# Banded attention heads of a two-layer trunk: values as weights in two column halves, both query groups in one unit

## The chip, the cores and the metric

One core of a Trainium2 chip runs the whole program. The metric is the device time of one execution in microseconds (us), the median of three runs. The core has a matrix engine (TensorE, PE in the profile; PEld is its weight load), a vector engine (VectorE, DVE), an activation engine (ScalarE, ACT), GpSimd (POOL), and a queue that issues the transfers (SyncE, SP). Operands lie in SBUF; TensorE writes its results to PSUM banks of 128 x 512 floats.

## The reference

A diffusion trunk of two layers over 256 latent tokens (x) and 256 context tokens (h). Each layer is a SwiGLU sub-layer, a token mixing with three groups of heads, and a second SwiGLU sub-layer, each between norms whose shifts, scales and gates come from conditioning vectors.

```
uv_x, qb_x, qc_x, kb_x, vb_x, kc_x, vc_x = jnp.split(ax @ w_in[l], SPLITS, axis=-1)
...
o_a = chunk_gmlp(uv_x, gmlp_v_gain[l], gmlp_w_s[l], gmlp_b_s[l])
o_b = diff_post(diff_attention_latent(qb_x, k_all, v_all, lam), diff_subln[l], lam_init)
o_c = swa_latent(qc_x, kc_x, vc_x, kc_h, vc_h, sink)
mix_x = jnp.concatenate([o_a, o_b, o_c], axis=-1) @ w_out[l]
x = adaln_out(x, mix_x, norm_post[l, 1], mod_x[:, 5], 1.0)
```

The change is in o_c, the banded heads: four query heads of 64 columns, head kv*2+g with two key/value heads kv and two query groups g. A latent query block of 128 tokens reads 512 keys (latent and context), a context block the 256 context keys. A sink logit joins each softmax. In the last layer only the latent tokens are mixed.

## The kernel before

Weights come from HBM through a staging ring of three tiles (`stg`) and are split into a rounded part and its remainder (`hi` by ACT, L240; `lo` by DVE or POOL, L101). Products of split operands take three passes of TensorE: L250 and L254 where weights are stationary and tokens move, L263, L269 and L271 in `acc3_multi`, with tokens stationary in the output projection. Full-precision products (scores, transposes, probabilities times values) use plain float32 tiles; one such matmul leaves two records in the trace, a transpose one.

The mixing is written as a long main line of projections and output products, into which small units are interleaved. A unit is a generator: it emits some instructions, then yields a delay on a virtual clock that counts TensorE columns (`tick`), and goes on when the clock has passed the delay. `T_SOFT`, `T_SOFTC` and `T_TURN` are such delays, and `pace` spaces the starts. A scheduler then fixes one order for each engine; at run time each engine takes its own order strictly in turn.

`unit_c(tb, g, box)` handles token block tb and group g: scores of kv 0 and 1 (L865, contraction over 64 rows), mask, row maximum (L874), exponential with row sum (ACT, L876), the sink's exponential (L878), reciprocal; after T_SOFT, `soft_T` turns each probability tile in 128x128 pieces (L781, copied to SBUF by L783); after T_TURN, L895 multiplies with the turned probabilities stationary (128 columns of weights) and 64 columns of values moving, and ACT copies the result, scaled by the reciprocal, into its quarter of `oc` (L899). When both groups of a block are through, `finish_c` turns `oc` (L1010), and writes Yh and Yl, the split operand of the output projection, rows 6 and 7 (L1014, L1015).

There are four blocks in layer 0 (tb 2 and 3 with 256 keys, tb 0 and 1 with 512) and two in layer 1 (512 keys). `unit_b` (L797, L781, L818) does the same for the differential heads, `post_b` (L846, L850, L851) their norm and turn. `spatial` (L929) is the gated group: two matmuls with 64-column weights write the two partition halves of one bank. `done` and `residual` (L1082, L1083, L422, L439, L444, L447) follow an output block of 128 tokens; `turn_y` (L461, L466, L471) makes the input of the next sub-layer.

Ring of six tiles of 512 columns, tag "p": probabilities, gate temporaries, gate rows, and more; ring of seven tiles of 256 columns, tag "sq". PSUM: four `pa`, two `pb`, two `pc` banks.

Of the kernel before, what the change touches and what calls it, by code (L numbers as in the profile page):

```python
# [37 lines left out]
T_SOFT, T_SOFTC, T_TURN, T_POST = 4.5, 3.5, 1.5, 3.0  # L38
# [25 lines left out]
def trunk(ctx: ExitStack, tc: tile.TileContext, x, c, cx, c_ctx, w_mod, b_mod, norm_pre, norm_post,  # L64
# [623 lines left out]
    def mixing(l, streams, qstreams, nxt):  # L688
# [166 lines left out]
        def unit_c(tb, g, box):  # L855
            k0, k1 = keys_of(tb)
            n = k1 - k0
            nkb = n // P
            mx = sm.tile([P, 2], F32, tag="mx", name=nm("mx"))
            ss = sm.tile([P, 4], F32, tag="ss4", name=nm("ss"))  # L860
            rs = sm.tile([P, 2], F32, tag="rs", name=nm("rs"))
            sc = [pa(), pa()]
            p = [half("p"), half("p")]
            for kv in range(2):
                nc.tensor.matmul(sc[kv][:, 0:n],  # L865
                                 lhsT=CU[64 * kv:64 * kv + 64, 1 + g, tb * P:(tb + 1) * P],
                                 rhs=CU[64 * kv:64 * kv + 64, 0, k0:k1], start=True, stop=True)
# [11 lines left out]
            nc.vector.tensor_tensor(rs, ss[:, 0:2], ss[:, 2:4], op=ALU.add)
            nc.vector.reciprocal(rs, rs)  # L880
            tick(1536)
            yield T_SOFT
            pT = []
            for kv in range(2):
# [6 lines left out]
            for kv in range(2):  # L891
                hd = kv * 2 + g
# [107 lines left out]
        def units_c(tb, w):  # L1000
            return [(2.0 * w, unit_c(tb, g, boxes[tb])) for g in range(2)]

        def finish_c(tb):
            while pending[("u", tb)]:
                yield 0.4
            oc = boxes[tb][0]
            yield T_TURN
            t = pa()
            for i in range(2):
                nc.tensor.transpose(t[:, i * P:(i + 1) * P], oc[:, i * P:(i + 1) * P], ident)  # L1010
# [318 lines left out]
```

## Time and profile before

| what | value |
|---|---|
| median of three runs | 1762.15 us (1761.32 to 1762.53) |
| profiled execution, time | 1762.98 us |
| profiled execution, span of its instructions | 1761.2 us |
| TensorE busy | 1722.4 us (98%) |
| VectorE busy | 1190.4 us (68%) |
| ScalarE busy | 696.3 us (40%) |
| mean granted TensorE clock | 0.997 |

The span runs from the first to the last instruction; the 1.8 us around it are start and end. Busy is the union of an engine's records. TensorE's matmuls overlap each other in the records, so that its pace is read from one start to the next. The mixing of layer 0 lies at some 465 to 640 us of the span, that of layer 1 at some 1455 to 1570 us.

### The profile page before, as it was taken

What the parts mean: (1) busy time and instruction counts of PE and PEld (TensorE: products, weight loads), DVE (VectorE), ACT (ScalarE), POOL (GpSimd) and SP (SyncE); (2) the same over time, 40 slices, a digit from 0 to 9 for tenths busy, and PEclk for the clock granted to TensorE, in tenths of its full rate; (3) what the DMA queues carried; (4) which work ended last, traced back from release to release, by engine and by line L of the source; (5) the groups of instructions that cost most, each with busy time, mean ns of one, the idle gap of its engine ahead of it and who ended that gap; (6) DMA issues with size and microseconds to landing.
All of it is one profiled execution on the core that took longest, in us unless ns stands there. A gap on an engine that the chain in (4) does not pass through costs nothing.

```text
span 1761.2 us, 24837 instructions
## 1 busy us (share of the span) xinstructions
PE 1722.4 (98%) x9663; PEld 1449.9 (82%) x9663; DVE 1190.4 (68%) x2174; ACT 696.3 (40%) x1480; POOL 168.9 (10%) x185
## 2 busy tenths in 40 slices
PE   7999999999999999999999999999999999999998
PEld 5788888879977789888888898888888897689997
DVE  4876876775667576768766576777864756765555
ACT  4332322244376562333232442332223526655443
POOL 0000000021322120000000210000001321010000
PEclk9999999999999999999999999999999999999999
DMA  9654554543131143445545233655544133226552
GB/s 336 207 173 160 188 197 144 167 150 109 60 103 52 57 137 125 162 163 189 191 144 185 75 120 123 205 178 191 180 144 167 48 108 120 73 90 197 192 191 84
DMA packets 197105, 259.20 MB, mean 147 GB/s; under 512 B 8234, under 2 KB 132348, under 8 KB 196988
## 3 DMA queue, kind: packets, MB, share of 16 engines
q1 hardware_dynamic: 195452, 257.56, 44.3%
q8 instruction: 76, 1.25, 0.3%
q14 instruction: 41, 0.34, 0.1%
q0 software_dynamic: 1536, 0.05, 0.0%
HBM read 256.49 MB, written 1.10 MB: 146 GB/s over the span
## 4 chain that ended last, share of the span: by engine, by line
PE 63%; DVE 7%; ACT 2%; issue 2%; POOL 1%; DMA 1%; POOLq 0%; DVEq 0%; ACTq 0%
PE pa L250 19%; PE pa L254 9%; PE pb L269 4%; PE pb L271 4%; PE pb L263 4%; PE pa L263 4%; PE pa L271 4%; PE pa L269 4%; PE pb L250 3%; DVE lo L101 2%; PE pb L254 1%; PE pa L797 1%; PE pc L818 1%; PE pc L895 1%; DVE S L439 1%
## 5 line engine op out<-in xcount | busy, mean ns | idle before, releaser
L101 DVE TENSOR_TENSOR lo<-stg,hi 128x512 fp32r<-128x512 f32 (+3 forms) x476 | 367.0, 807 | 192.5 <-ACT hi L240 122.8
L240 ACT ACTIVATE hi<-stg 128x512 fp32r<-128x512 f32 (+3 forms) x496 | 318.4, 702 | 329.6 <-PE pa L263 97.2
L250 PE MATMUL pa<-Yh,hi 128*128 128x512 f32 (+1 forms) x1168 | 415.0, 365 | 0.0
L250 PE MATMUL pa<-Yl,hi 128*128 128x512 f32 (+1 forms) x1168 | 413.8, 364 | 0.0
L357 DVE SCALAR_TENSOR_TENSOR acc<-stg,sT,acc 128x512 f32<-128x512 f32 x448 | 305.2, 743 | 4.0 <-DMA stg<-in_w_mod_dram 4.0
L254 PE MATMUL pa<-Yh,lo 128*128 128x512 f32 (+1 forms) x1168 | 257.8, 363 | 0.0
L250 PEld LDWEIGHTS pa<-Yh,hi 128*128 128x128 f32 x1168 | 220.5, 189 | 36.6 <-issue 2.9
L250 PEld LDWEIGHTS pa<-Yl,hi 128*128 128x128 f32 x1168 | 220.5, 189 | 35.0 <-issue 1.2
L254 PEld LDWEIGHTS pa<-Yh,lo 128*128 128x128 f32 x1168 | 202.4, 189 | 34.3
L570 ACT ACTIVATE Uh<-ha 128x512 fp32r<-128x512 f32 (+1 forms) x92 | 50.7, 551 | 296.4 <-DVE ha L568 296.4
L263 PE MATMUL pb<-hi,Ul 128*128 128x512 f32 x400 | 156.9, 392 | 0.0
L271 PE MATMUL pb<-lo,Uh 128*128 128x512 f32 x400 | 155.9, 390 | 0.8 <-DVE lo L101 0.8
L269 PE MATMUL pb<-hi,Uh 128*128 128x512 f32 x400 | 155.8, 391 | 0.1
L568 DVE TENSOR_TENSOR ha<-ha,pa 128x512 f32<-128x512 f32 (+1 forms) x91 | 53.0, 583 | 79.5 <-PE pa L254 79.0
L269 PE MATMUL pa<-Yh,hi 128*128 128x256 f32 x368 | 92.0, 285 | 0.0
L271 PE MATMUL pa<-Yl,hi 128*128 128x256 f32 x368 | 91.3, 283 | 0.0
L271 PEld LDWEIGHTS pb<-lo,Uh 128*128 128x128 f32 x400 | 75.1, 188 | 16.6 <-DVE lo L101 1.3
L263 PEld LDWEIGHTS pb<-hi,Ul 128*128 128x128 f32 x400 | 75.1, 188 | 16.5 <-issue 1.2
L269 PEld LDWEIGHTS pb<-hi,Uh 128*128 128x128 f32 x400 | 75.2, 188 | 16.0 <-DVE Z L503 0.5
L566 ACT ACTIVATE ht<-pa 128x512 f32<-128x512 f32 (+1 forms) x91 | 46.3, 510 | 104.1 <-PE pa L254 81.8
L379 POOL DMA_DIRECT2D gate<-gr x48 | 24.3, 513 | 603.7 <-DVE gr L376 535.3
L567 DVE SCALAR_TENSOR_TENSOR ha<-ht,pa 128x512 f32<-128x512 f32 (+1 forms) x91 | 52.9, 581 | 37.2 <-ACT ht L566 36.4
(299 smaller groups left out, 2732.4 us busy)
## 6 DMA issues: line engine op xcount, KB each, us to landing
stg<-in_w_mod_dram SPq DMA_DIRECT2D x64, 1024.0 KB, 5.0
stg<-in_ffn_w_gate_dram SPq DMA_DIRECT2D x42, 1024.0 KB, 5.2
stg<-in_ffn_w_up_dram SPq DMA_DIRECT2D x42, 1024.0 KB, 5.1
stg<-in_ffn_w_down_dram SPq DMA_DIRECT2D x32, 1024.0 KB, 5.0
stg<-in_w_in_dram SPq DMA_DIRECT2D x14, 1024.0 KB, 4.8
stg<-in_ffn_w_down_dram SPq DMA_DIRECT2D x16, 768.0 KB, 4.4
mst<-in_w_mod_dram SPq DMA_DIRECT2D x16, 512.0 KB, 7.6
stg<-in_w_out_dram SPq DMA_DIRECT2D x8, 1024.0 KB, 6.4
```

Of the source, the lines that this page charges most:

```text
L101: eng.tensor_tensor(lo, full, f32(hi), op=ALU.subtract)
L240: nc.scalar.activation(hi[:, a:b, :], v[:, a:b, :], AF.Copy)
L250: nc.tensor.matmul(o, lhsT=ah, rhs=r, start=(i == 0), stop=(i == n - 1))
L254: nc.tensor.matmul(o, lhsT=al, rhs=bh, start=(i == 0), stop=(i == n - 1))
L263: nc.tensor.matmul(o, lhsT=al, rhs=bh, start=False, stop=last, skip_group_check=True)
L269: nc.tensor.matmul(o, lhsT=ah, rhs=bh, start=(first and k == 0), stop=False, skip_group_check=True)
L271: nc.tensor.matmul(o, lhsT=ah, rhs=bl, start=False, stop=False, skip_group_check=True)
L357: nc.vector.scalar_tensor_tensor(a, v[:, k, :], sc, a, op0=ALU.mult, op1=ALU.add)
L566: nc.scalar.activation(t, g, AF.Tanh, scale=0.5)
L567: nc.vector.scalar_tensor_tensor(a, t, 1.0, g, op0=ALU.add, op1=ALU.mult)
L568: nc.vector.tensor_tensor(a, a, u, op=ALU.mult)
L570: nc.scalar.activation(uh, a, AF.Copy)
```

## The change

One unit now handles a block with both groups. It makes the four probability tiles, DVE multiplies each by its reciprocal (L885), and the turned pieces of both groups stand side by side in one PSUM bank (L896: two key blocks x two groups). Values are stationary with 64 columns, 256 columns of turned probabilities move (L903), and kv 0 and kv 1 write partitions 0 to 63 and 64 to 127 of one bank. The result is already turned, in the order (kv, d) by (g, token): the turning of `oc` falls away, and the rows of w_out that meet it are loaded in the same order, through two transfers of 64 partitions each (`out_stage`). gelu2's temporaries move from the "p" ring to the "sq" ring.

```diff
-T_SOFT, T_SOFTC, T_TURN, T_POST = 4.5, 3.5, 1.5, 3.0
+T_SOFT, T_SOFTC, T_TURN, T_POST = 4.5, 6.5, 1.5, 3.0
...
-        def unit_c(tb, g, box):
+        def unit_c(tb, w, box):
...
-            yield T_SOFT
-            pT = []
-            for kv in range(2):
-                pT.append(soft_T(p[kv], nkb))
-                tick(nkb * 288)
-            yield T_TURN
-            if not box:
-                box.append(wk.tile([P, 256], F32, tag="sq", name=nm("oc"), bufs=7))
-            oc = box[0]
-            for kv in range(2):
-                hd = kv * 2 + g
-                o = pc()
-                for kb in range(nkb):
-                    nc.tensor.matmul(o[:, 0:64], lhsT=pT[kv][:, kb * P:(kb + 1) * P],
-                                     rhs=VG[:, k0 // P + kb, 512 + kv * 64:512 + kv * 64 + 64],
-                                     start=(kb == 0), stop=(kb == nkb - 1))
-                tick(nkb * 320)
-                nc.scalar.activation(oc[:, hd * 64:hd * 64 + 64], o[:, 0:64], AF.Copy,
-                                     scale=rs[:, kv:kv + 1])
+                for kv in range(2):
+                    nc.vector.tensor_scalar(p[g, kv][:, 0:n], p[g, kv][:, 0:n], rs[:, kv:kv + 1], None,
+                                            op0=ALU.mult)
+                tick(1536)
+                yield T_SOFTC if g else w * pace[0]
+            o = pc()
+            for kb in range(0, nkb, 2):
+                pT = []
+                for kv in range(2):
+                    t = pa()
+                    for i in range(4):
+                        c0 = (kb + i // 2) * P
+                        nc.tensor.transpose(t[:, i * P:(i + 1) * P], p[i % 2, kv][:, c0:c0 + P], ident)
+                    pT.append(wk.tile([P, 512], F32, tag="a", name=nm("pT")))
+                    nc.scalar.activation(pT[kv], t, AF.Copy)
+                tick(2304)
+                yield T_TURN
+                for i in range(2):
+                    for kv in range(2):
+                        nc.tensor.matmul(o[64 * kv:64 * kv + 64, 0:256],
+                                         lhsT=VG[:, k0 // P + kb + i, 512 + kv * 64:576 + kv * 64],
+                                         rhs=pT[kv][:, i * 256:(i + 1) * 256], start=(kb + i == 0),
+                                         stop=(kb + i == nkb - 1))
+                tick(2560)
+            oc = wk.tile([P, 256], F32, tag="sq", name=nm("oc"), bufs=7)
+            nc.scalar.activation(oc, o[:, 0:256], AF.Copy)
+            box.append(oc)
...
-            xs, q = half("gx")[:, 0:n], half("gq")[:, 0:n]
+            xs, q = [wk.tile([P, 256], F32, tag="sq", name=nm(t), bufs=7) for t in ("gx", "gq")]
...
-            return [(2.0 * w, unit_c(tb, g, boxes[tb])) for g in range(2)]
+            return [(4.0 * w, unit_c(tb, 2.0 * w, boxes[tb]))]
...
+        def out_stage(blocks, c0, ncol):
...
+            nc.sync.dma_start(v[:, k0:k0 + n, :],
+                              w_out[l, r0:r0 + n * P, cs].rearrange("(k p) c -> p k c", p=P))
+            if 6 in blocks:
+                k0 = blocks.index(6)
+                for kv in range(2):
+                    r0 = (6 + kv) * P
+                    nc.sync.dma_start(v[64 * kv:64 * kv + 64, k0:k0 + 2, :],
+                                      w_out[l, r0:r0 + P, cs].rearrange("(g d) c -> d g c", g=2))
+            return v
```

**TensorE, layer 0, the first of the two 512-key blocks, before.** L865 is a score product, L895 probabilities times values of one kv, L781 a turn, L263 to L271 the output projection of the context tokens.

```order
L263 MATMUL pb_5257<-hi_5146,Yl 128x512
L865 MATMUL pa_5382<-CU_3759 128x512
L865 MATMUL pa_5383<-CU_3759 128x512
L269 MATMUL pb_5257<-hi_5146,Yh 128x512
L271 MATMUL pb_5257<-lo_5147,Yh 128x512
L895 MATMUL pc_5402<-VG_3223,pT_5367 128x64 x4
L895 MATMUL pc_5408<-VG_3223,pT_5374 128x64 x4
L781 MATMUL pa_5414<-ident,p_5326 128x128 x4
L781 MATMUL pa_5421<-ident,p_5327 128x128 x4
```

The same block in the changed order, its two groups of L903 (p_5196 and p_5256 are the probabilities of kv 0, p_5297 belongs to the next block; L939 is `spatial`):

```order
L903 MATMUL pc_5360<-pT_5366,VG_3223 64x256
L903 MATMUL pc_5360<-pT_5373,VG_3223 64x256
L903 MATMUL pc_5360<-pT_5366,VG_3223 64x256
L903 MATMUL pc_5360<-pT_5373,VG_3223 64x256
...
L896 MATMUL pa_5466<-ident,p_5297 128x128
L903 MATMUL pc_5360<-pT_5413,VG_3223 64x256
L939 MATMUL pc_5449<-wsT_3220,VG_3223 64x128 x2
...
L903 MATMUL pc_5360<-pT_5420,VG_3223 64x256
L903 MATMUL pc_5360<-pT_5413,VG_3223 64x256
L903 MATMUL pc_5360<-pT_5420,VG_3223 64x256
```

Two sets of eight 64-column products per block became two groups of four 256-column products. The first group stands together; in the second one product stands alone and three follow later.

**ScalarE, layer 0, the second 512-key block, after.** L879 is the exponential of a probability tile, L881 the sink's, L898 the copy of a turned bank; p_5297 and p_5299 are the first group of the second block, p_5380 and p_5382 the other group.

```order
L879 ACTIVATE p_5297,ss_5293<-pa_5295,mx_5292 128x512
L881 ACTIVATE ss_5293<-sink_3202,mx_5292 128x1
L898 ACTIVATE pT_5366<-pa_5361 128x512
L898 ACTIVATE pT_5373<-pa_5368 128x512
L881 ACTIVATE ss_5376<-sink_3202,mx_5375 128x1 x2
L879 ACTIVATE p_5299,ss_5293<-pa_5296,mx_5292 128x512
L879 ACTIVATE p_5380,ss_5376<-pa_5378,mx_5375 128x512
L898 ACTIVATE pT_5413<-pa_5408 128x512
```

The second exponential of the first group stands behind the sink exponentials of the other group.

**TensorE, layer 1, from the last scores of the second block on, before.** L846 turns the differential heads' output; the last row is the first of the second output block and needs their Yh.

```order
L865 MATMUL pa_13283<-CU_12221 128x512
L865 MATMUL pa_13284<-CU_12221 128x512
L781 MATMUL pa_13301<-ident,p_13216 128x128 x4
L781 MATMUL pa_13308<-ident,p_13217 128x128 x4
L263 MATMUL pb_13188<-hi_13017,Yl 128x256
L263 MATMUL pb_13188<-Yh,Yl 128x256 x6
L846 MATMUL pa_13322<-ident,CU_12221 128x128 x4
L263 MATMUL pb_13188<-Yh,Yl 128x256 x2
L895 MATMUL pc_13353<-VG_11787,pT_13306 128x64 x4
L781 MATMUL pa_13365<-ident,p_13285 128x128 x4
L781 MATMUL pa_13372<-ident,p_13286 128x128 x4
L895 MATMUL pc_13359<-VG_11787,pT_13313 128x64 x4
...
L269 MATMUL pb_13396<-hi_12837,Yh 128x512
```

And after, where L868 is the score product:

```order
L868 MATMUL pa_13228<-CU_12171 128x512
L263 MATMUL pb_13130<-hi_12905,Yl 128x256
L263 MATMUL pb_13130<-Yh,Yl 128x256 x7
L846 MATMUL pa_13255<-ident,CU_12171 128x128 x4
L263 MATMUL pb_13130<-Yh,Yl 128x256
L896 MATMUL pa_13285<-ident,p_13152 128x128
L896 MATMUL pa_13292<-ident,p_13154 128x128
L269 MATMUL pb_13349<-hi_12789,Yh 128x512
L271 MATMUL pb_13349<-lo_12790,Yh 128x512
...
L271 MATMUL pb_13349<-lo_12790,Yh 128x512
L896 MATMUL pa_13285<-ident,p_13229 128x128
```

The eight products and sixteen turns that stood between the last scores and the second output block are two turns now. Between the two pieces shown, 15 products of 256 columns and 3 of 512 follow, then the first turn of the other group, p_13229.

**VectorE, layer 1, the same stretch, after.** L422 to L447 are the residual and norm of the first output block, L885 the new multiplication.

```order
L422 SCALAR_TENSOR_TENSOR v_13268<-ss_12927 128x1
L1099 TENSOR_TENSOR zg_13263<-pb_13130,VG_11737 128x512
L439 SCALAR_TENSOR_TENSOR S<-zg_13127,r_13269,S 128x512
L439 SCALAR_TENSOR_TENSOR S<-zg_13263,r_13269,S 128x512
L882 TENSOR_TENSOR rs_13226<-ss_13225 128x2
L851 SCALAR_TENSOR_TENSOR Yl<-pa_13255,gsub_5771,Yh 128x4x128
L883 RECIPROCAL rs_13226<-rs_13226 128x2
L422 SCALAR_TENSOR_TENSOR v_13277<-ss_13274 128x1
L885 TENSOR_SCALAR p_13229<-p_13229,rs_13226 128x512
```

The multiplication of p_13229 stands behind the residual and behind a second L422.

**ScalarE, layer 1, start of the last sub-layer, before** (L240 splits a weight tile, the last one is the fourth weight tile of that sub-layer; L444 is the square of the residual):

```order
L1082 ACTIVATE zg_13445,ss_13351<-pb_13396 128x512
L240 ACTIVATE hi_13534<-stg_13532 128x512 x4
L1082 ACTIVATE zg_13497,ss_13351<-pb_13448 128x512
L240 ACTIVATE hi_13556<-stg_13554 128x512
L444 ACTIVATE yt_13500,ss_13508<-S 128x512
L444 ACTIVATE yt_13501,ss_13508<-S 128x512
L240 ACTIVATE hi_13556<-stg_13554 128x512 x3
```

and after:

```order
L1098 ACTIVATE zg_13374,ss_13283<-pb_13349 128x512
L240 ACTIVATE hi_13463<-stg_13461 128x512 x4
L1098 ACTIVATE zg_13426,ss_13283<-pb_13377 128x512
L240 ACTIVATE hi_13485<-stg_13483 128x512 x4
L444 ACTIVATE yt_13429,ss_13437<-S 128x512
L444 ACTIVATE yt_13430,ss_13437<-S 128x512
```

All four pieces of the fourth tile now stand ahead of L444; before, three stood behind it.

## Rows read from the trace of the kernel before

**Rows 1.** The page, part 1: busy us, share of the span, instructions.

```profile
PE 1722.4 (98%) x9663; PEld 1449.9 (82%) x9663; DVE 1190.4 (68%) x2174; ACT 696.3 (40%) x1480; POOL 168.9 (10%) x185
```

**Rows 2.** Busy us by stage: start:end, length, PE, PEld, DVE, ACT, POOL, clock, DMA share, GB/s.

```profile
480.00:620.00 140.00, 133.34 (x870) 105.59 (x869) 95.14 (x255) 91.39 (x275) 25.73 (x20) 1.00 0.21 70
1460.00:1580.00 120.00, 111.61 (x734) 90.28 (x733) 88.06 (x194) 78.53 (x208) 20.27 (x18) 0.99 0.31 104
```

**Rows 3.** Groups by line and shape, count: busy us, mean ns, idle before.

```profile
L895 PE MATMUL pc<-VG,pT 128*128 128x64 f32 x160 | 20.2, 274 | 1.2 <-ACT pT L783 1.2
```

**Rows 4.** TensorE in order of time, layer 0: start us, us, instruction, records.

```profile
526.11 1.10 PE L895 MATMUL pc<-VG,pT 128*128 128x64 f32 x8 [0.65 <-ACT pT L783]
527.15 0.70 PE L865 MATMUL pa<-CU 64*128 64x256 f32 x4
...
590.73 2.00 PE L895 MATMUL pc<-VG,pT 128*128 128x64 f32 x16
592.57 0.61 PE L846 MATMUL pa<-ident,CU 128*128 128x128 f32 x4
...
600.50 0.38 PE L1010 MATMUL pa<-ident,oc 128*128 128x128 f32 x2
600.81 0.44 PE L929 MATMUL pc<-wsT,VG 128*64 128x128 f32 x4
```

**Rows 5.** TensorE in order of time, layer 0: products in halves of the array.

```profile
544.82 0.44 PE L929 MATMUL pc<-wsT,VG 128*64 128x128 f32 x4
545.19 0.39 PE L250 MATMUL pb<-lo,Yh 128*128 128x256 f32 x1
...
588.83 1.97 PE L865 MATMUL pa<-CU 64*128 64x512 f32 x4
...
604.22 0.66 PE L929 MATMUL pc<-wsT,VG 128*64 128x128 f32 x8
604.80 0.50 PE L269 MATMUL pb<-hi,Yh 128*128 128x512 f32 x1
```

**Rows 6.** TensorE in order of time, layer 1: idle us before, and its releaser, in brackets.

```profile
1498.80 1.16 PE L846 MATMUL pa<-ident,CU 128*128 128x128 f32 x4 [1.37 <-ACT pT L783]
...
1505.89 0.66 PE L781 MATMUL pa<-ident,p 128*128 128x128 f32 x4 [1.03 <-ACT p L876]
...
1507.78 0.66 PE L781 MATMUL pa<-ident,p 128*128 128x128 f32 x4 [0.65 <-ACT p L876]
...
1542.59 1.10 PE L895 MATMUL pc<-VG,pT 128*128 128x64 f32 x8 [0.59 <-ACT pT L783]
```

**Rows 7.** Groups by line and shape on DVE and ACT.

```profile
L447 DVE TENSOR_SCALAR Z<-S,r 128x512 f32<-128x512 f32 x28 | 14.4, 552 | 9.1 <-POOL r L424 9.1
L899 ACT ACTIVATE oc<-pc,rs 128x64 f32<-128x64 f32 x24 | 7.4, 312 | 5.1 <-PE pc L895 4.8
```

**Rows 8.** PE, ACT and DVE in order of time, layer 1, after the last scores.

```profile
1536.49 1.13 PE L865 MATMUL pa<-CU 64*128 64x512 f32 x4
1539.65 0.69 ACT L876 ACTIVATE p<-pa,mx 128x512 f32<-128x512 f32 x1 [0.75 <-DVE mx L875]
1542.42 0.69 ACT L850 ACTIVATE Yh<-pa,gsub 128x512 fp32r<-128x512 f32 x1
1545.79 0.16 DVE L422 SCALAR_TENSOR_TENSOR v<-ss 128x1 f32<-128x1 f32 x1 [0.73 <-ACT yt L444]
```

**Rows 9.** ACT and PE in order of time, layer 1, start of the last sub-layer.

```profile
1566.81 1.65 ACT L240 ACTIVATE hi<-stg 128x512 fp32r<-128x512 f32 x3
1567.48 0.39 PE L269 MATMUL pa<-hi,Yh 128*128 128x256 f32 x1 [0.73 <-ACT hi L240]
1569.37 0.39 PE L271 MATMUL pa<-lo,Yh 128*128 128x256 f32 x1 [1.50 <-DVE lo L101]
```

**Rows 10.** Busy us by stage, as rows 2, the 4 us behind those waits.

```profile
1570.00:1574.00 4.00, 4.00 (x23) 4.00 (x23) 1.27 (x3) 1.07 (x3) 0.00 (x0) 0.57 0.56 154
```

**Rows 11.** The page, part 6: w_out transfers, KB each, median us from issue to landing.

```profile
stg<-in_w_out_dram SPq DMA_DIRECT2D x8, 1024.0 KB, 6.4
```

More of the change, by code (lines that the diff above doesn't have):

```diff
@@ L879, in unit_c @@
[L879 to L900 removed]
+            p = {}
@@ new lines, in unit_c @@
+            for g in range(2):
+                mx = sm.tile([P, 2], F32, tag="mx", name=nm("mx"))
+                ss = sm.tile([P, 4], F32, tag="ss4", name=nm("ss"))
+                rs = sm.tile([P, 2], F32, tag="rs", name=nm("rs"))
+                sc = [pa(), pa()]
+                for kv in range(2):
+                    p[g, kv] = half("p")
+                    nc.tensor.matmul(sc[kv][:, 0:n],
+                                     lhsT=CU[64 * kv:64 * kv + 64, 1 + g, tb * P:(tb + 1) * P],
+                                     rhs=CU[64 * kv:64 * kv + 64, 0, k0:k1], start=True, stop=True)
+                for kv in range(2):
+                    hd = kv * 2 + g
+                    if tb < 2:
+                        far = sc[kv][:, (1 - tb) * P:(2 - tb) * P]
+                        nc.vector.tensor_tensor(far, far, mask[:, tb, :], op=ALU.add)
+                    m = mx[:, kv:kv + 1]
+                    nc.vector.tensor_reduce(m, sc[kv][:, 0:n], axis=AX.X, op=ALU.max, negate=True)
+                    nc.vector.tensor_tensor(m, m, mp["nsk"][:, hd:hd + 1], op=ALU.min)
+                    nc.scalar.activation(p[g, kv][:, 0:n], sc[kv][:, 0:n], AF.Exp, bias=m,
+                                         accum_out=ss[:, kv:kv + 1])
+                    nc.scalar.activation(ss[:, 2 + kv:3 + kv], mp["sk"][:, hd:hd + 1], AF.Exp, bias=m)
+                nc.vector.tensor_tensor(rs, ss[:, 0:2], ss[:, 2:4], op=ALU.add)
+                nc.vector.reciprocal(rs, rs)
+                for kv in range(2):
[3 more added lines that the diff above has]
+                yield T_SOFTC if g else w * pace[0]
@@ new lines, in unit_c @@
+            o = pc()
[11 more added lines that the diff above has]
+                for i in range(2):
+                    for kv in range(2):
+                        nc.tensor.matmul(o[64 * kv:64 * kv + 64, 0:256],
[3 more added lines that the diff above has]
+                tick(2560)
@@ L1005, in finish_c @@
                 yield 0.4
[L1006 to L1010, printed above, removed]
-            tick(600)
-            tv = t[:, 0:256].rearrange("p (h q) -> p h q", h=2)
+            oc = boxes[tb][0].rearrange("p (g q) -> p g q", g=2)
             oh = Yh[:, 6:8, ycols(tb)]
-            nc.scalar.activation(oh, tv, AF.Copy)
-            split_lo(Yl[:, 6:8, ycols(tb)], tv, oh)
+            nc.scalar.activation(oh, oc, AF.Copy)
+            split_lo(Yl[:, 6:8, ycols(tb)], oc, oh)
         def open_posts(s):
@@ L1036, in out_rows @@
             def out_rows(kk):
-                v = wst.tile([P, 2048], F32, tag="stg", name=nm("stg")).rearrange(
-                    "p (k c) -> p k c", k=4)
-                for k0, n, r0 in ((0, 4, 256),) if kk == 0 else ((0, 2, 768), (2, 2, 0)):
-                    nc.sync.dma_start(v[:, k0:k0 + n, :],
-                                      w_out[l, r0:r0 + n * P, 0:512].rearrange("(k p) c -> p k c", p=P))
-                return split(v, 4, 512)
+                return split(out_stage((2, 3, 4, 5) if kk == 0 else (6, 7, 0, 1), 0, 512), 4, 512)
             def out_cols(c0, into=None):
-                return wchunk([(0, 256, w_out[l, :, c0:c0 + 256])], KB, 256, into=into)
+                return split(out_stage(range(KB), c0, 256), KB, 256, into=into)
             def oterms(w, tb, f0=0):
@@ L1128, in chunk @@
         def chunk(hf, i):
-            return wchunk([(0, 512, w_out[l, i * 512:(i + 1) * 512, hf * 512:(hf + 1) * 512])], 4, 512,
-                          share=True)
+            return split(out_stage(range(4 * i, 4 * i + 4), hf * 512, 512), 4, 512, share=True)
         def oterms(ws, tb):
```

24 lines of the change are left out of this document (7 added, 17 removed).

## The prediction

> **What bounds the kernel now.** I read the page's busy table first: TensorE is busy for 1722.4 of 1761.2 us [rows 1], so time is gained by taking work from TensorE, or one of its few waits, and lost by giving it new waits. The order of instructions of before and after differs only inside the two mixing stages, so I cut the span there [rows 2]: TensorE is idle for 6.7 us of 140 in layer 0 and 8.4 of 120 in layer 1. DVE is busy for 95.1 and 88.1 us, ACT for 91.4 and 78.5. Neither bounds a stage on average, but at two thirds to three quarters busy, and strictly in order, either can be late at a given point. Then I looked at the timeline of TensorE for the pace of the products concerned, and at each wait longer than 0.5 us.
>
> **What TensorE is relieved of.** A busy sum over 160 records of L895 [rows 3] mixes in overlap, so I go by one start to the next. Sixteen records (eight products, one group of a 512-key block) take 592.57 - 590.73 = 1.84 us; eight (a 256-key block) take 527.15 - 526.11 = 1.04 us; the two turns of `oc` take 600.81 - 600.50 = 0.31 us [rows 4]. Four blocks with 512 keys: 4 x (2 x 1.84 + 0.31) = 16.0. Two with 256: 2 x (2 x 1.04 + 0.31) = 4.8. Together 20.7 us. A record costs 0.115 us although only 64 columns move.
>
> The Trainium skill (TensorE: Matmul & The Clock Gate, LDWEIGHTS) gives a weight load as columns/1.2 ns, 107 ns for 128 columns; the rows agree within a tenth: by that rule the 160 records would cost 17.1 us, by the rows 18.9 with the first and last of each set.
>
> **What TensorE gets.** Ten groups of four products (two for each 512-key block, one for each 256-key block), 64 columns of weights, 256 moving. No row shows this shape. The nearest is `spatial`, which also writes the two partition halves of one bank: two products of 128 columns take 545.19 - 544.82 = 0.37 us, four take 604.80 - 604.22 = 0.58 [rows 5]. So one more pair costs 0.21 us, and a stretch of such products 0.16 us to enter and leave. With 256 columns a pair costs 0.42, a group 2 x 0.42 + 0.16 = 1.00 us. In the changed order four of the ten groups are torn: one product alone (0.42 + 0.16), later three (0.84 + 0.16), 1.58 us. Sum: 6 x 1.00 + 4 x 1.58 = 12.3. TensorE gains 20.7 - 12.3 = 8.4 us. The sixteen or eight turns of probabilities are as many as before.
>
> Bounds. If the two halves ran one after the other, a group would cost 4 x 0.42 + 0.16 = 1.84, ten of them 18.4, and 2.3 us would be gained. That this happens is seen once: two score products in separate row halves took from 588.83 to 590.73, 1.90 us, which is 0.95 for each 512 columns [rows 4, 5]. If nothing were paid for entering and leaving, 10 x 0.84 + 4 x 0.42 = 10.1, and the gain would be 10.6.
>
> The Trainium skill (TensorEngine Tiling, Tiling Modes) speaks against the change here: switching between tiling modes drains the engine, and each of the 14 stretches switches twice. The rows of `spatial` show that drain as the 0.16 us; with it the gain is 8.4, without it 10.6, and I take the rows.
>
> **Other engines.** DVE gets 24 multiplications. The nearest row is a scaling by a column at 0.552 us for 512 columns [rows 7]; halved for the eight with 256 columns that makes 16 x 0.55 + 8 x 0.28 = 11 us, beside 45 + 32 us of idle DVE in the two stages [rows 2]. ACT loses 24 scaled copies of 0.312 us, 7.5 us [rows 7], and gets six of the double size. Both cost nothing by themselves, as long as TensorE has main-line products between the softmax and the turns; without that cover each multiplication delays a turn by 0.55 us. The w_out tiles come through two or three transfers more for each staged tile, on SP's queue; a transfer of 1 MB lands 6.4 us after its issue [rows 11], and the projections that use them stand tens of us later. I take zero. If that cover were gone, it would be some 6 us once. gelu2's move to the other ring changes no durations.
>
> **Waits that go.** Five waits of TensorE belong to the old units: 0.65 before L895 [rows 4], and 1.37, 1.03, 0.65 and 0.59 [rows 6], together 4.3 us. Each is a turn or a product that follows too closely on ACT's exponential or copy, or the bank it frees. In the changed order other rows stand at these places, so I take them off whole; since new ones of the kind will come in stretches that I did not follow row by row, I put back 2.0 (between 0 and 4.3, near the middle).
>
> **Waits that come.** (a) Layer 1, after the last scores of the second block. Scores end at 1536.49 + 1.13 = 1537.6, and the first exponential starts at 1539.65, 2.1 later; L850, which writes the Yh that the second output block begins with, ends at 1543.11, 3.5 after that exponential [rows 8]. In the changed order the same instructions stand ahead of L850, less one copy of about 0.6: it ends 2.1 + 2.9 = 5.0 us after the scores. TensorE has eight products of 256 columns, four turns, one product and two turns to do till then, about 1.9 us by the 0.12 us of one such row. So it waits 3.1 us, where eight products and sixteen turns covered it before. Next, the turn of p_13229: its multiplication stands on DVE behind the second L422, which ended 6.3 us after the first exponential [rows 8]; 2.1 + 6.3 + 0.55 is 9.0, or 8.3 without the ACT copies that then stood ahead of L444. TensorE gets there at 5.0 + 0.46 + 15 x 0.12 + 0.70 = 8.0. I take 0.6. Last, the copy of the product, the copy to Yh and a weight split between them on ACT take some 1.8 us, beside 1.0 us of products: 0.8. Together 4.5 us (between 1 and 7).
>
> (b) Layer 0, second 512-key block: the second exponential stands behind the sink exponentials of the other group, and both multiplications behind it. That puts the first turn of p_5297 about as late as TensorE's rows in between take, some 5 to 6 us after the last scores: 1.5 us (0 to 3).
>
> (c) At the start of the last sub-layer TensorE waits 0.73 and 1.50 us for ACT's three late pieces of the fourth weight tile and their remainders [rows 9]. In the changed order all four pieces stand ahead of L444: minus 2.2 (0 to -2.2). Behind these waits the granted clock was 0.57 for 4 us [rows 10]: the lower level, 1.2 GHz, for most of that stretch, which cost 1.7 us. It may go with them, or come back behind wait (a); I count neither.
>
> **Sum.** -8.4 - 4.3 + 2.0 + 1.5 + 4.5 - 2.2 = -6.9 us. Against the profiled execution, 1762.98, that is 1756.1. The median, 1762.15, lies 0.8 below that execution, so I predict 1755.3. A difference of 0.2%, 3.5 us, is about what a measurement of this kernel can tell from none.
>
> **Rivals.**
> 1. The halves do not run side by side. The gain of TensorE is 2.3 instead of 8.4, the rest stands: 1761.4, within 0.2%. For it speaks the serial pair at 588.83, against it that all rows of L929 overlap. 6 in 100.
> 2. The gain is given back in waits: (a) at its upper bound of 7, the old waits replaced by as many (4.3 instead of 2.0), and the slow clock at both places. 1755.3 + 2.5 + 2.3 + 1.7 = 1761.8, no change that can be told. DVE's load in layer 1 speaks for it. 13 in 100.
> 3. Slower: the ring "p". A block now holds four of its six tiles till both groups are turned, and the gate rows hold two more. The next block's exponentials then wait on ACT for the first block's turns, and everything behind them on ACT waits too: copies of turned banks, and the splits of w_out tiles that the output projection needs. It decides from the point at which this costs TensorE 5.2 us more in each layer (6.9 + 3.5 over two): 1766 or more. For it speaks the changed order in layer 0, where an exponential already stands behind the other group's; against it that TensorE has fourteen products between. 8 in 100.
> 4. More is gained: (a) and (b) mostly covered, 1 and 0 us, and the slow clock gone: 1755.3 - 3.5 - 1.5 - 1.7 = 1748.6. 16 in 100.
>
> **How the numbers follow.** The forecast has 57 in 100, between 1752 and 1758.5. With rival 4 the faster side has 73, rivals 1 and 2 make 19 for no change, rival 3 makes 8. The range 1750 to 1761 takes in most of 4 and about half of 1 and 2.
>
> **What would show it.** L903 in the profile after: 80 records, in groups of eight from one start to the next 1.0 us; 1.8 would show rival 1. TensorE's busy time 8 us lower. A wait of about 3 us before L269 of pb in layer 1, with ACT's Yh as releaser, would show (a); none would show rival 4. The waits for L240 and L101 at the start of the last sub-layer gone would show (c). Exponentials that wait on ACT for a turn on TensorE, with TensorE idle behind them, would show rival 3. I am wrong if the sum of TensorE's waits in the two stages, 15 us now, is above 23 or below 11.

## The result, and the profile after

The changed kernel takes 1771.55 us (median of 6 runs, 1769.17 to 1779.39) beside 1761.91 for the kernel before (6 runs): ratio 1.0065, 95% interval 1.0042 to 1.0089. The ratio is of the means; the changed kernel is slower by 0.65%. The profiled execution takes 1769.17, 6.2 us more than that of before. Three executions of those listed further down (one of the kernel before, two of e11_hp_soft) took 2425 us or more and are left out of every figure.

The first part of the page, and the two mixing stages as in [rows 2]:

```profile
PE 1722.0 (97%) x9571; PEld 1440.2 (81%) x9571; DVE 1197.4 (68%) x2198; ACT 694.2 (39%) x1458; POOL 168.7 (10%) x185
```

```profile
480.00:620.00 140.00, 128.80 (x796) 96.50 (x795) 98.64 (x268) 87.11 (x252) 26.46 (x20) 0.98 0.21 66
1460.00:1580.00 120.00, 108.89 (x655) 82.99 (x654) 86.81 (x195) 75.51 (x193) 19.71 (x18) 0.94 0.31 97
```

TensorE has 92 instructions less, yet is as long busy as before [rows 1]: part of that time runs at half the clock. Its idle time in the two windows is 260.0 - 237.7 = 22.3 us; before it was 15.0 [rows 2]. The clock column has fallen from 1.00 and 0.99 to 0.98 and 0.94.

The new product, as a group of rows and in order of time (a whole group of eight records in layer 0 and what follows it, then a torn one):

```profile
L903 PE MATMUL pc<-pT,VG 128*64 128x256 f32 x80 | 13.4, 395 | 0.0
```

```profile
531.18 1.08 PE L903 MATMUL pc<-pT,VG 128*64 128x256 f32 x8
532.20 1.13 PE L797 MATMUL pa<-QK 64*128 64x512 f32 x4
...
613.59 0.65 PE L903 MATMUL pc<-pT,VG 128*64 128x256 f32 x2
614.16 0.44 PE L896 MATMUL pa<-ident,p 128*128 128x128 f32 x2
614.53 1.08 PE L903 MATMUL pc<-pT,VG 128*64 128x256 f32 x6
615.54 0.44 PE L896 MATMUL pa<-ident,p 128*128 128x128 f32 x2
```

Eight records (four products) take 1.02 us from one start to the next, and all six whole groups 1.01 or 1.02. 1.00 was forecast for halves side by side and 1.84 for one after the other, so they do run side by side. A torn group takes 0.57 + 1.01 = 1.58, as forecast.

TensorE's waits, layer 0 and then layer 1 (idle us and its releaser in brackets):

```profile
539.65 0.39 PE L250 MATMUL pb<-hi,Yh 128*128 128x256 f32 x1 [2.78 <-ACT gq L915]
567.24 0.76 PE L781 MATMUL pa<-ident,p 128*128 128x128 f32 x4 [3.83 <-DVE p L808]
576.00 0.66 PE L781 MATMUL pa<-ident,p 128*128 128x128 f32 x4 [0.27 <-DVE p L808]
586.09 1.16 PE L818 MATMUL pc<-VG,pT 128*128 128x128 f32 x8 [0.29 <-ACT pT L783]
597.28 0.50 PE L269 MATMUL pb<-hi,Yh 128*128 128x512 f32 x1 [1.05 <-ACT hi L240]
599.71 0.50 PE L271 MATMUL pb<-lo,Yh 128*128 128x512 f32 x1 [1.60 <-POOL lo L101]
...
1506.33 0.79 PE L263 MATMUL pb<-hi,Yl 128*128 128x512 f32 x1 [3.17 <-DVE Yl L851]
1544.59 0.33 PE L896 MATMUL pa<-ident,p 128*128 128x128 f32 x1 [0.56 <-ACT p L879]
1546.84 0.50 PE L269 MATMUL pb<-hi,Yh 128*128 128x512 f32 x1 [1.93 <-ACT Yh L850]
1569.35 0.39 PE L271 MATMUL pa<-lo,Yh 128*128 128x256 f32 x1 [1.03 <-DVE lo L101]
1571.05 0.49 PE L271 MATMUL pa<-lo,Yh 128*128 128x256 f32 x1 [0.48 <-DVE lo L101]
```

The five stretches just behind the long ones, and one behind the last two (same columns as [rows 2], the clock is the third number from the end):

```profile
540.00:544.00 4.00, 4.00 (x24) 3.80 (x22) 3.52 (x13) 2.96 (x9) 0.00 (x0) 0.57 0.01 4
567.50:571.50 4.00, 4.00 (x17) 2.23 (x16) 2.37 (x6) 2.58 (x6) 0.00 (x0) 0.57 0.97 288
1506.00:1510.00 4.00, 3.67 (x7) 1.62 (x8) 2.57 (x9) 4.00 (x12) 0.00 (x0) 0.54 0.13 45
1510.00:1513.50 3.50, 3.50 (x15) 2.23 (x13) 3.50 (x9) 2.63 (x6) 0.00 (x0) 0.55 0.00 0
1547.00:1551.00 4.00, 4.00 (x19) 3.81 (x20) 3.55 (x10) 1.39 (x4) 0.67 (x1) 0.57 0.00 0
1571.00:1575.00 4.00, 3.95 (x20) 3.95 (x21) 3.87 (x9) 1.39 (x4) 0.55 (x1) 0.57 0.54 147
```

In each the clock is at the lower level, 1.2 GHz, for most of the time, which costs some 4 x (1 - 0.57) = 1.7 us. Before, the two stages held one such stretch [rows 10], now six. Over the whole span the clock loss is span x (1 - mean granted clock): 1761.2 x 0.003 = 5.3 us before, 1767.4 x 0.007 = 12.4 after. The clock is listed to 0.001, so one execution's loss is known to about 0.9 us.

So the profiled execution's +6.2 us divides into waits +7.3, clock +7.1, and TensorE's work, by what is left, -8.2.

The six runs differ by the clock in the main. Their clock losses are 12.4, 19.6, 15.9, 8.8, 23.1 and 8.8 us (mean 14.8); without them the times lie between 1755 and 1761. Of the 10.2 us between the fastest and the slowest, 7.2 are clock. The 91 runs of the kernel before that were listed with the experiments lose 1.8 to 8.8, mean 5.1.

How a wait arises, at 539.65. TensorE's scores are the row at 532.20 above; here VectorE and ScalarE in order of time:

```profile
535.71 0.43 DVE L931 TENSOR_TENSOR VG<-VG,r 128x256 f32<-128x256 f32 x1 [1.12 <-POOL r L930]
536.69 0.29 DVE L841 TENSOR_SCALAR CU<-CU,r 128x128 f32<-128x128 f32 x1 [0.55 <-POOL r L839]
537.56 0.67 DVE L800 TENSOR_REDUCE mx<-pa 128x1 f32<-128x512 f32 x1
538.27 0.69 ACT L802 ACTIVATE p<-pa,mx 128x512 f32<-128x512 f32 x1 [2.80 <-DVE mx L800]
539.21 0.38 ACT L915 ACTIVATE gq<-pb 128x256 f32<-128x256 f32 x1
```

The scores are there at 533.3. Their maximum (L800) starts 4.2 us later: among the rows ahead of it on VectorE are two norms that wait 1.12 and 0.55 us for GpSimd's power. The exponential (L802) waits with it; behind the exponential stands the square (L915) that frees the bank TensorE wants. The Trainium skill (TensorE: Matmul & The Clock Gate, Architectural detail: the array is 16× 32×32, not 1× 128×128) says that ScalarE and VectorE take their queues strictly in order; these rows agree, 2.80 us of an idle ScalarE with a ready square behind the head. The waits at 567.24 and 1506.33 are of the same make: the differential softmax's p (L808) and the remainder Yl stand on VectorE behind a gate norm that waits 1.06 and 0.92 us for GpSimd. That is under a third of either wait (3.83 and 3.17); in the rest VectorE mostly works on other rows that stand ahead. The first of the two:

```profile
566.10 0.42 DVE L931 TENSOR_TENSOR VG<-VG,r 128x256 f32<-128x256 f32 x1 [1.06 <-POOL r L930]
566.44 0.74 DVE L808 SCALAR_TENSOR_TENSOR p<-p,rs,p 128x512 f32<-128x512 f32 x1
```

### The profile page after: what moved, and what is told of

The parts are those of the page before. It is cut to its first block, busy times and chain, and to the rows that moved or that the text cites. A ratio compares the mean times of both kernels' runs of the same rounds, so it can differ in the third digit from the quotient of the medians.

```text
span 1767.4 us, 24659 instructions
## 1 busy us (share of the span) xinstructions
PE 1722.0 (97%) x9571; PEld 1440.2 (81%) x9571; DVE 1197.4 (68%) x2198; ACT 694.2 (39%) x1458; POOL 168.7 (10%) x185
## 4 chain that ended last, share of the span: by engine, by line
PE 57%; DVE 6%; ACT 2%; issue 1%; POOL 1%; DMA 0%; POOLq 0%; DVEq 0%; ACTq 0%
PE pa L250 19%; PE pa L254 9%; PE pb L269 4%; PE pb L263 4%; PE pb L271 4%; PE pa L263 4%; PE pa L271 4%; PE pa L269 4%; DVE lo L101 1%; PE pb L250 1%; PE pa L797 1%; PE pb L254 1%; PE pc L367 1%; PE pc L903 1%; DVE Yh L471 1%
## 5 line engine op out<-in xcount | busy, mean ns | idle before, releaser
L101 DVE TENSOR_TENSOR lo<-stg,hi 128x512 fp32r<-128x512 f32 (+3 forms) x476 | 366.9, 809 | 191.4 <-ACT hi L240 121.0
L240 ACT ACTIVATE hi<-stg 128x512 fp32r<-128x512 f32 (+3 forms) x496 | 318.2, 701 | 325.4 <-PE pa L263 100.1
L263 PE MATMUL pb<-hi,Ul 128*128 128x512 f32 x400 | 157.1, 393 | 0.0
L271 PE MATMUL pb<-lo,Uh 128*128 128x512 f32 x400 | 156.1, 390 | 0.8 <-DVE lo L101 0.8
L271 PE MATMUL pa<-Yl,hi 128*128 128x256 f32 x368 | 91.3, 283 | 0.0
L271 PEld LDWEIGHTS pb<-lo,Uh 128*128 128x128 f32 x400 | 75.1, 188 | 16.7 <-DVE lo L101 1.3
L263 PEld LDWEIGHTS pb<-hi,Ul 128*128 128x128 f32 x400 | 75.1, 188 | 16.4 <-issue 1.2
```

Source lines behind the costliest of these rows:

```text
L101: eng.tensor_tensor(lo, full, f32(hi), op=ALU.subtract)
L240: nc.scalar.activation(hi[:, a:b, :], v[:, a:b, :], AF.Copy)
L263: nc.tensor.matmul(o, lhsT=al, rhs=bh, start=False, stop=last, skip_group_check=True)
L271: nc.tensor.matmul(o, lhsT=ah, rhs=bl, start=False, stop=False, skip_group_check=True)
```

## The experiments

Theories. **O**: the loss comes from the places that rows take in the in-order queues; these decide how long single waits are. **C**: what makes a long wait dear is the lower clock behind it. **L**: the 24 multiplications are too much for VectorE. **R**: the 256-column ring is short for gelu2's temporaries. Each kernel was executed 5 to 12 times. "Waits" is TensorE's idle time in the two windows above in the one profiled execution, "clock" the mean loss of all runs of that kernel, "rest" the mean time without both.

| kernel | median us | ratio to before, 95% interval | waits | clock | rest |
|---|---|---|---|---|---|
| before (91 runs, mean 1762) | | | 15.0 | 5.1 | 1742 |
| changed | 1771.55 | 1.0065 [1.0042, 1.0089] | 22.3 | 14.8 | 1736 |
| e1_gelu_only | 1770.12 | 1.0047 [1.0035, 1.0060] | 16.0 | 12.7 | 1741 |
| e2_gelu_old | 1773.27 | 1.0070 [1.0057, 1.0082] | 23.0 | 13.8 | 1737 |
| e3_no_mul | 1764.01 | 1.0015 [1.0006, 1.0024] | 22.0 | 9.1 | 1733 |
| e4_soft35 | 1764.78 | 1.0015 [1.0006, 1.0024] | 20.5 | 10.4 | 1734 |
| e4_soft80 | 1771.76 | 1.0065 [1.0046, 1.0084] | 20.3 | 17.4 | 1736 |
| e5_act_mul | 1770.70 | 1.0051 [1.0039, 1.0063] | 21.4 | 12.7 | 1737 |
| e7_fill | 1773.05 | 1.0061 [1.0049, 1.0073] | 17.3 | 9.6 | 1746 |
| e8_soft35_fill | 1765.63 | 1.0020 [1.0011, 1.0029] | 18.0 | 10.3 | 1737 |
| e9_two_units | 1766.82 | 1.0032 [1.0019, 1.0044] | 23.7 | 8.2 | 1735 |
| e9b_two_units_ring | 1761.05 | 0.9994 [0.9985, 1.0003] | 21.6 | 5.9 | 1734 |
| e10_hp_copy | 1755.40 | 0.9962 [0.9950, 0.9973] | 17.8 | 4.6 | 1733 |
| e11_hp_soft | 1761.7 | 0.9996 [0.9986, 1.0005] | 18.5 | 7.0 | 1736 |
| e13_before_hp | 1762.66 | 0.9998 [0.9990, 1.0007] | 14.9 | 8.2 | 1739 |
| e14_after_hp | 1767.13 | 1.0037 [1.0022, 1.0051] | 21.8 | 14.7 | 1732 |
| e17_hp_no_mul | 1754.78 | 0.9958 [0.9946, 0.9970] | 15.0 | 8.4 | 1731 |

### The parts of the change

**e1_gelu_only**, on the kernel before; **e2_gelu_old** is its reverse on the changed kernel.

```diff
-            xs, q = half("gx")[:, 0:n], half("gq")[:, 0:n]
+            xs, q = [wk.tile([P, 256], F32, tag="sq", name=nm(t), bufs=7) for t in ("gx", "gq")]
```

> The kernel before with one part of the change, the gate activation's two temporaries in the 256-column ring. Theory O (order): the new waits of the changed kernel come from the places that the joined unit's rows take in the queues of VectorE and ScalarE, so this part alone moves few rows and the time stays within 3 us of 1762. Theory R (ring): the temporaries now compete with the banded heads' output tiles and the copies stall; then 1766 or more. Theory L (load: the 24 multiplications on VectorE) expects 1762 as O does.

> The changed kernel with the gate activation's temporaries back in the 512-column ring that also holds the probabilities. Theory O: the same waits at the same places, 1768 to 1778. Theory R: the waits for the gate activation go and with them the slow clock behind them, 1765 or less. If instead the ring of the probabilities is what is short, it gets slower than the changed kernel, 1780.

The part that I had costed at nothing costs 8 us alone. In numbers R is met and O is not. But R's mechanism is not seen: gelu2's copies wait for TensorE's product alone, none for a buffer of the ring, and the waits sum to only 1.0 us more than before. They are lumped: before, 1.37, 1.03 and 0.65 us between 1498 and 1508 [rows 6]; now

```profile
1501.83 1.12 PE L846 MATMUL pa<-ident,CU 128*128 128x128 f32 x4 [3.38 <-ACT pT L783]
```

and three stretches at the lower level in a row:

```profile
1500.00:1503.50 3.50, 1.67 (x9) 1.68 (x9) 3.35 (x7) 3.09 (x6) 0.27 (x1) 0.53 0.00 0
1503.50:1507.00 3.50, 3.50 (x18) 3.50 (x18) 2.73 (x7) 0.55 (x3) 0.74 (x1) 0.50 0.90 289
1507.00:1510.50 3.50, 3.50 (x18) 3.50 (x18) 0.03 (x1) 1.57 (x6) 0.00 (x0) 0.51 0.05 16
```

Its clock loss is 12.7 us against 5.1; with 1.0 of waits that is the 8 us. Taking the part back (e2) gains nothing, where R expected 1765 or less. R falls.

**e3_no_mul** leaves out the 24 multiplications (L885); **e5_act_mul** gives them to ScalarE.

```diff
-                    nc.vector.tensor_scalar(p[g, kv][:, 0:n], p[g, kv][:, 0:n], rs[:, kv:kv + 1], None,
-                                            op0=ALU.mult)
+                    nc.scalar.activation(p[g, kv][:, 0:n], p[g, kv][:, 0:n], AF.Copy,
+                                         scale=rs[:, kv:kv + 1])
```

> The changed kernel without the 24 multiplications on VectorE (the probabilities stay unscaled, so the banded heads are not normalised); line numbers are kept. Theory L: VectorE gets 11 us back in the two mixing stages, the sum of TensorE's waits there falls from 22 us to 15 or less and most of the stretches at the lower clock go: 1755 to 1760. Theory O: the multiplications are a small part of what stands ahead of the late rows, so at most 3 us are gained: 1766 to 1772.

> The changed kernel with the 24 multiplications on ScalarE instead of VectorE. Theory L (VectorE is short): the awaited softmax and norm steps come earlier, TensorE's waits fall from 22.8 us by 4 or more. Theory O: the waits move to other places with about the same sum, and the time is set by how many of them are long enough to bring the lower clock: anywhere from 1760 to 1775, with waits plus clock loss accounting for the difference to the changed kernel within 2 us.

1764.0 lies between the two theories' figures. The waits did not fall (22.0), against L; the clock loss did, 14.8 to 9.1, and the rest by 3. So 7.5 us are gained without these 24 rows, more than O allows, and why the clock loss fell is not shown. On ScalarE nothing is gained. L is out for the waits.

**e4_soft35** and **e4_soft80** change one constant of the planner.

```diff
-T_SOFT, T_SOFTC, T_TURN, T_POST = 4.5, 6.5, 1.5, 3.0
+T_SOFT, T_SOFTC, T_TURN, T_POST = 4.5, 3.5, 1.5, 3.0
```

> The changed kernel with the planner's time between the second scores and their turns at 3.5 us instead of 6.5, so nothing changes but the order. Theory O: the waits stand at other places and the time moves by 4 us or more, either way. Theories L and R: the same work on the same engines, so the same time within 3 us, 1767 to 1775.

> The changed kernel with the planner's time between the second scores and their turns at 8.0 us instead of 6.5. If 6.5 is too short for the softmax, waits fall and the time is under 1766; if the longer time only moves rows, the waits stay at 20 to 25 us and the time moves by the number of slow stretches, 1.7 us each.

With 3.5 the same work is 6.8 us faster; with 8.0 as slow as with 6.5. Nothing but the order differs, as O says. Waits are about 20 in both, the clock loss is 10.4 and 17.4.

### Filling the waits

**e7_fill** puts turns of the unit matrix ahead of four long waits of the changed kernel, **e8_soft35_fill** ahead of one of e4_soft35's.

```diff
+        def warm(t, n):
+            for _ in range(n):
+                nc.tensor.transpose(t[:, 0:P], ident, ident)
```

> The changed kernel with useless turns of the unit matrix (into banks that the next product overwrites) placed in TensorE's queue just ahead of four of its long waits: 20 at the 2.78 us wait of layer 0, 28 at the one of 3.83, 22 at the one of 3.17 in layer 1 and 12 at the one of 1.93. 82 turns are 9.5 us of TensorE, laid into waits that sum to 11.7 us. Theory C (clock): it is the lower clock behind a long wait that costs, 1.7 us for each of five of the six stretches; with TensorE kept at work these stretches go and the time falls by up to 8.5 us, 1760 to 1765. Theory O without the clock: the rows awaited come at the same time, so nothing is gained: 1768 to 1778. If TensorE were what is short, the turns would cost their 9.5 us: 1780.

> The kernel of the shorter planner time (3.5 us) with 22 useless turns ahead of the one long wait of layer 1 (3.3 us), behind which its clock fell for two stretches that cost 3.4 us. Theory C: 3 us less than that kernel, 1760 to 1763, so about the time of the kernel before. Without C: 1764 to 1767.

Both missed C's figures and came out in the ranges written for no gain. In e7 the clock held at all four places, even at the first, where a wait of 2.57 us was left:

```profile
542.00:546.00 4.00, 2.76 (x24) 2.60 (x26) 2.54 (x9) 2.86 (x9) 0.00 (x0) 1.00 0.02 4
569.00:573.00 4.00, 3.77 (x24) 2.76 (x25) 3.48 (x8) 2.79 (x7) 1.01 (x1) 1.00 1.05 296
1508.00:1512.00 4.00, 3.23 (x16) 1.70 (x14) 3.81 (x13) 3.49 (x11) 0.00 (x0) 1.00 0.55 193
1550.00:1554.00 4.00, 3.38 (x24) 2.98 (x23) 3.48 (x9) 2.06 (x6) 1.20 (x2) 1.00 0.00 0
```

but two lower stretches each came at 600 and 1518, behind waits of 1.04 and 1.60, and 1.15 and 1.33; and only 5.0 of the 9.5 us of turns fell into waits (22.3 to 17.3), the rest was added. In e8 the filled wait shrank from 3.3 to 0.92 us, but one of 1.66 came 3 us later, and the clock loss stayed (10.4, now 10.3). Over its runs e7's clock loss is 9.6 for 14.8, as C says; as a remedy filling is worth nothing here.

But a wait does not fix the stretch behind it. The wait of 1.93 before the second output block stands unchanged in e2_gelu_old, e4_soft80 and e14_after_hp, without a stretch; in e14 the one of 3.18 before L263 has none either (the 4 us behind these two in e14, clock 1.00):

```profile
1506.50:1510.50 4.00, 3.66 (x15) 2.03 (x17) 3.81 (x13) 4.00 (x12) 0.00 (x0) 1.00 0.14 48
1548.00:1552.00 4.00, 3.74 (x25) 3.23 (x26) 3.55 (x9) 1.80 (x5) 0.67 (x1) 1.00 0.00 0
```

And the pair that brought two stretches in e7 (1.04 and 1.60) stands in the changed kernel as 1.05 and 1.60 with none. So no single place shows C, and how many stretches a set of waits brings is known only as a mean over runs.

### The product without the joined unit

**e9_two_units** keeps each group a unit of its own, as before, and takes the new product from it; **e9b_two_units_ring** adds gelu2's move.

```diff
-            for kv in range(2):
-                hd = kv * 2 + g
-                o = pc()
-                for kb in range(nkb):
-                    nc.tensor.matmul(o[:, 0:64], lhsT=pT[kv][:, kb * P:(kb + 1) * P],
-                                     rhs=VG[:, k0 // P + kb, 512 + kv * 64:512 + kv * 64 + 64], ...
+            o = pc()
+            for kb in range(nkb):
+                for kv in range(2):
+                    nc.tensor.matmul(o[64 * kv:64 * kv + 64, 0:P],
+                                     lhsT=VG[:, k0 // P + kb, 512 + kv * 64:576 + kv * 64],
+                                     rhs=pT[kv][:, kb * P:(kb + 1) * P], ...
+            nc.scalar.activation(oc[:, g * P:(g + 1) * P], o[:, 0:P], AF.Copy)
```

> The new product without the joined unit: each group of a block stays a unit of its own, as before, with its two probability tiles scaled on VectorE and four pairs of 128-column products (values as weights) instead of four of 256; the gate activation's temporaries stay in the 512-column ring. TensorE's work falls as in the change (about 8 us by the rows), the rows of the other engines keep nearly the order of before. Theory O (order, through waits and the clock behind them): waits near the 15.5 us of before, one to three slow stretches, 1755 to 1760. Theory L (the multiplications are what makes the softmax late): waits over 20 us, 1764 or more.

> The same with the gate activation's temporaries in the 256-column ring. Alone on the kernel before that part cost 8 us, nearly all of it by slow stretches. If the ring itself stalls something, it costs as much here: 1763 to 1768. If it only moved rows into a worse order there, the difference to the kernel with two units is of either sign and made of slow stretches, 1.7 us each.

The waits sum to no less (23.7, 21.6), against O's figure, but the longest is 2.92 us for 3.83, and the clock loss is 8.2 and 5.9. In numbers e9 is where L put it (waits over 20, 1764 or more); e9b and e10 below keep the same multiplications and are 5.8 and 11.4 us faster, so the time is not theirs. The ring's move, which cost 8 us on the kernel before, gains 5.8 here: of either sign, so order. From the changed kernel to e9b the means differ by 12.4 us: waits make 0.7, clock 8.9 and the rest 2.8. The split transfers of w_out are the same in both, so they are not what costs.

e9b's longest wait is for a copy of a turned tile. ScalarE and TensorE in order of time:

```profile
1535.65 1.09 PE L781 MATMUL pa<-ident,p 128*128 128x128 f32 x8
1538.05 0.69 ACT L877 ACTIVATE p<-pa,mx 128x512 f32<-128x512 f32 x1 [1.05 <-DVE mx L876]
1540.34 0.59 ACT L783 ACTIVATE pT<-pa 128x512 f32<-128x512 f32 x1
1540.99 1.97 PE L898 MATMUL pc<-pT,VG 128*64 128x128 f32 x14 [2.92 <-ACT pT L783]
```

The tile was turned at 1536.7; its copy stands behind the next unit's exponentials, which wait for VectorE.

**e10_hp_copy** puts the copies ahead, **e11_hp_soft** instead the maximum and the exponential.

```diff
-            nc.scalar.activation(pT[:, 0:nkb * P], t[:, 0:nkb * P], AF.Copy)
+            with tc.high_priority():
+                nc.scalar.activation(pT[:, 0:nkb * P], t[:, 0:nkb * P], AF.Copy)
```

> Two units and the 256-column ring, with the copies of turned probabilities put ahead of other work in ScalarE's queue (scheduler's high priority). In the trace of the two units the longest wait, 2.9 us in layer 1, is for such a copy: its turn had ended over 3 us before, but it stands behind two exponentials of the next unit that wait for VectorE. Theory O: with the copy ahead of them that wait and its two slow stretches (3.4 us) go, 1755 to 1759, faster than both kernels. If other waits take their place, 1760 to 1764.

> Two units and the 256-column ring, with the maximum, its minimum with the sink and the exponential of the banded heads ahead of other work in the queues of VectorE and ScalarE. Theory O: the waits for a softmax shrink and those for gate and norm steps grow; the sum stays at 20 to 24 us and the time within 3 us of the two units' 1761, by the number of slow stretches.

e10 beats both kernels: 1755.4, 0.4% below before. Its page has PE at

```profile
PE 1710.6 (98%) x9651; PEld 1436.1 (82%) x9651; DVE 1197.2 (68%) x2198; ACT 692.8 (40%) x1468; POOL 167.6 (10%) x185
```

11.8 us less than [rows 1]. The clock of the two profiled executions (losses of 3.5 and 5.3) makes 1.8 of it; the rest is less work for TensorE, seen now that the clock is up. Both copies now start right behind the turns (1530.70, two in 1.09 us), and the wait behind them is gone. e11 gains nothing (1761.7, as O expected); its waits, 18.5, came out under O's 20 to 24, and the wait for the copy is still there, 3.29 us.

**e13_before_hp** and **e14_after_hp** put the copies ahead in the kernel before and in the changed one (there also L898); **e17_hp_no_mul** is e10 without the multiplications.

> The kernel before with nothing changed but the copies of turned probabilities put ahead of other work in ScalarE's queue. If the place of the copies is a gain of its own, 1755 to 1759, and the new product has brought nothing in the kernel that beat both. If the copies only give back what the new product's order lost, the kernel before has little to gain: 1759 to 1764, and the 7 us are the product's.

> The changed kernel with the copies of turned probabilities, of both kinds of heads, put ahead of other work. Theory O with the joined unit as the place of the loss: its long waits are for a gate activation, a differential softmax, a remainder and an output, none of them such a copy, so at least three of the long waits stay and the time is 1766 to 1774. If the copies were the whole of it: 1755 to 1760.

> The kernel with two units, the 256-column ring and the copies ahead, without the 24 multiplications (the banded heads are not normalised). Theory L: its waits fall from 18.5 us to 15 or less, and it is 3 us or more faster than 1755.4. Theory O: waits move by less than 3 us either way, 1753 to 1758.

In the kernel before the copies bring nothing (0.9998), so the 7 us of e10 need more than the copies: the new product, or the ring's move with them (the kernel before with both moves was not run). In the changed kernel its four long waits stay, though the copies are ahead:

```profile
PE pa L781 <- DVE p L809: 4.0, 1, 4.0
PE pb L250 <- ACT gq L917: 2.8, 1, 2.8
...
PE pb L263 <- DVE mx L879: 3.2, 1, 3.2
...
PE pb L269 <- ACT Yh L851: 1.9, 1, 1.9
```

(releaser, us in total, times, longest). They belong to the joined unit's order: with two units and the same copies (e10) the first is 1.9, the second and third are gone, and only the last is as long (2.4). Without the multiplications e10 gains 0.6 us, within the intervals of both: waits fall by 2.7, to the 15.0 that L named, and the clock takes it back.

## Why the prediction was wrong

The forecast was -6.9 us; the profiled execution shows +6.2.

- **TensorE's work, -8.4: right in the main.** The ten new groups sum to 12.3 us by their starts, as forecast. The old rows sum to 19.4, not 20.7: 1.84 and 1.04 were the longest of their kinds (1.70 to 1.84, 0.91 to 1.04). So the gain is 7.2 by the starts; left over above is -8.2, and the clock's rounding is as large as the difference. "Rest" in the table is 1731 to 1737 in each kernel with the new product (e7's fillers apart), 1739 to 1742 in those without. Rival 1 is refuted. The sign that TensorE's busy time falls by 8 did not show (0.4): the lower clock lengthened the rows.
- **Waits that go, -4.3: right as far as it went.** Of the five only 0.45 us is left (before L846, at 1498.16).
- **(a) 4.5 us at the tail of layer 1: right in place, too large.** 0.56 + 1.93 = 2.5; the wait for the output's copy did not come.
- **(b) 1.5 us in layer 0:** no wait for p_5297's turn; at that place TensorE waits 2.65 for a w_out tile's split (597.28, 599.71) that stands on ScalarE behind a sink exponential (L881) which waits 1.12 us for VectorE:

```profile
595.99 0.29 ACT L881 ACTIVATE ss<-sink,mx 128x1 f32<-128x1 f32 x1 [1.12 <-DVE mx L878]
596.19 1.99 ACT L240 ACTIVATE hi<-stg 128x1024 fp32r<-128x1024 f32 x2
```

That is the path rival 3 named, without its cause: the exponential waits for VectorE's maximum, not for a tile of the ring.
- **(c) -2.2: nearly right.** The four waits from 1559.96 on summed to 3.4, the two left sum to 1.5, 1.9 less. They are for VectorE's remainders (L101); the slow stretch stayed behind them.
- **The step that failed first: "since new ones of the kind will come in stretches that I did not follow row by row, I put back 2.0 (between 0 and 4.3, near the middle)".** In such stretches 2.78 came at 539.65, 3.17 at 1506.33, and 0.99, 0.15 and 0.94 between 1516.98 and 1519.47: 8.0 for 2.0. I forecast 16.5 us of waits in the two stages and 22.3 came; by my own last sentence anything up to 23 was allowed.
- **The step that failed most: "I count neither"**, of the lower clock. I took it for a single event. Six stretches instead of one are 8.5 us in the two stages (7.1 over the span, since the execution of before lost one more near its start). The sum of the waits does not tell the price, as is seen between 560 and 590. Before:

```profile
563.28 0.66 PE L781 MATMUL pa<-ident,p 128*128 128x128 f32 x4 [0.61 <-DVE p L808]
567.26 1.16 PE L818 MATMUL pc<-VG,pT 128*128 128x128 f32 x8 [0.76 <-ACT pT L783]
572.72 0.66 PE L781 MATMUL pa<-ident,p 128*128 128x128 f32 x4 [1.50 <-DVE p L808]
584.05 1.16 PE L818 MATMUL pc<-VG,pT 128*128 128x128 f32 x8 [1.53 <-ACT pT L783]
```

4.4 us at full clock; after, 3.83 + 0.27 + 0.29 = 4.4 us, and the clock falls behind the 3.83. Rival 2 had the right kind (waits and slow clock) at a fifth of the clock's price, 1.7 us.
- **"gelu2's move to the other ring changes no durations" and zero for edits on other engines:** no duration changed, yet the move alone cost 8 us by order, and without the 24 multiplications the changed kernel is 7.5 us faster (e3). Zero holds for an engine's time, not for its queue.

What stays open: which waits bring a slow stretch (one of 2.10 in e4_soft35, at 582.33, has none, and the same 1.93 has one in one kernel and none in three); why O's figures missed in e1 and e9, so that it names the cause but does not forecast the size; and how far any order of the joined unit could go, of which three delays were run. A norm without GpSimd's power was not tried.

## What to carry to other kernels

Here TensorE was 98% busy and the gain of the cheaper product was real, but it was paid out only where the rows that moved with it made few long waits. So list each place at which an awaited row stands behind one that waits for a third engine, and price a long wait with the slow stretch that may follow it, 1.7 us here. What paid here was to change the product without regrouping the units around it, and then to put the copies that TensorE waits for ahead in their queue. Judge an edit by its order on every engine, even where it moves only a buffer.

## What the runs showed of the hardware that was not expected

The lower clock came in stretches that cost some 1.7 us each, up to three in a row (e1_gelu_only), also while TensorE was fully busy (1503.50 to 1510.50 there). The same wait at the same place was followed by one in one kernel's execution and by none in another's (1.93 us: changed kernel and e14_after_hp). The number of stretches differs between executions of one program: 8.8 to 23.1 us of loss in six runs of the changed kernel, which is most of its spread.
